# Three of four chunk outputs and their group norms moved into the state recurrence of a hybrid RWKV-7 and MLA decoder

## The chip, the core and the metric

One core of a Trainium2 chip. The metric is the device time of one execution in microseconds (us); the kernel before has a median of 1591.6 us over 3 runs (1591.0 to 1593.85). Engines are called as in the profile: PE is TensorE (PEld its weight loads), DVE is VectorE, ACT is ScalarE, POOL is GpSimd, SP is SyncE, which issues the transfers.

## The reference

Two decoder layers on 512 tokens of width 1024, then a norm. Each layer has a mixer of two branches, RWKV-7 and MLA attention, and a gated MLP. What the change touches is the RWKV branch: a state of 64x64 for each of 8 heads runs over all tokens, each token's output is read from the state, and the output is normed within its head.

```
def step(state, inp):
    r_t, w_t, k_t, v_t, a_t, b_t = inp
    sa = jnp.einsum('bhij,bhj->bhi', state, a_t)
    state = (state * w_t[:, :, None, :] + sa[..., None] * b_t[:, :, None, :]
             + v_t[..., None] * k_t[:, :, None, :])
    y_t = jnp.einsum('bhij,bhj->bhi', state, r_t)
    return state, y_t
...
mu = jnp.mean(y, axis=-1, keepdims=True)
var = jnp.mean(jnp.square(y - mu), axis=-1, keepdims=True)
y = ((y - mu) * lax.rsqrt(var + LNX_EPS)).reshape(B, S, RWKV_DIM).astype(dt) * lnx_w + lnx_b
...
return (y + bonus) * gate
```

The MLA branch is plain causal attention of 8 heads over the 512 tokens (scores, softmax, values). It doesn't depend on the recurrence; both branches meet behind their output projections.

## The kernel before

Activations lie transposed, 128 channels by 512 tokens. Every large projection is a chain of matmuls of 128x512 in three terms, high part by high part, high by low, low by high (`mm3`, L246 to L248), on weights that SP streams in and that ACT and DVE split into two parts (L201, L202). These matmuls are most of PE's work.

In each layer's mixer the 512 tokens are 8 chunks of 64. What couples tokens inside a chunk is prepared ahead (AR, AM, BT, Z). Then comes the recurrence, a loop over the chunks, c = 0 to 7, and each step is a chain between PE and DVE: PE reads the state (L785), DVE adds to `xs` (L789), PE multiplies with the chunk's inverse (L795), DVE writes the result to Z (L798), PE multiplies with BT (L804), DVE adds the decayed state from POOL (L811) to the new state `St` (L812). Between these three groups of small matmuls `filler()` puts matmuls of two projections that don't depend on the recurrence, two `mm3` at a time; it has six such pieces, which last until step 2.

Behind the loop `outputs()` forms the RWKV outputs of four chunk pairs: `chunk_out(i)` multiplies the states by AR (L833) and Z by AM (L841) into one pair of banks `xy`, and ACT copies the sum to Z (L844). `norms()` runs the group norm of each pair: DVE sum, mean and subtraction (L852 to L854), square on ACT (L855), sum and mean on DVE (L856, L857), power -0.5 on POOL (L858) and a product on POOL (L863). `transposed()` turns the four normed pairs with PE (`yop`, L869), and DVE scales and gates them (L874, L875) for the output projection. `heads(p)`, p = 0 to 3, is the attention of two heads each: scores into one of the two banks of the tag `sc` (L929), minimum on DVE (L932), exponential on ACT (L935), reciprocal on DVE (L936), scaling on ACT (L937), transposes on PE (L940) into one bank `pt`, a copy on DVE or ACT (L942), product with the values on PE (L947).

What sets the order: the recurrence is written in a block in which PE's instructions keep the order of the program among themselves. All else is ordered ahead of time by a scheduler that goes by the order of the program, by buffers and by its own costs, one fixed list for each engine; instructions of other parts of the program may be put between those of the block. So in the kernel before a good part of `heads(0)` and of the projections for it lies between the recurrence's steps 2 to 7.

```
for f in (outputs, norms, lambda: heads(0), lambda: heads(1), transposed, lambda: heads(2), lambda: heads(3)):
    f()
```

Of the kernel before, what the change touches and what calls it, by code (L numbers as in the profile page):

```python
# [9 lines left out]
F32 = mybir.dt.float32  # L10
F32R = mybir.dt.float32r
I32 = mybir.dt.int32
AF = mybir.ActivationFunctionType
# [12 lines left out]
LNX_EPS = 64e-5  # L26
# [132 lines left out]
def build(ctx, tc, x, pos, wst, vecd, constd, out):  # L159
# [265 lines left out]
    def mixer(l, ops, nrm, wks):  # L425
        with ExitStack() as mx:
# [220 lines left out]
            with pool(name=f"ti{l}", bufs=2) as ti, tc.manual_schedule(engines={PE.engine}):  # L647
# [120 lines left out]

                St = [None]
# [7 lines left out]
                for c in range(8):  # L777
# [3 lines left out]
                    if c:  # L781
# [5 lines left out]
                        filler()  # L787
# [29 lines left out]
            with pool(name=f"tb{l}", bufs=2) as tb:  # L817
# [6 lines left out]

                def chunk_out(i):
                    xy = xyt()
                    for p in range(4):
                        for e, hh in ((0, 0), (1, 1), (0, 1), (1, 0)):
                            c = 2 * i + e
                            ur, vr = rows(e)  # L830
                            k0 = 64 * hh
                            if c:
                                PE.matmul(xy[vr:vr + 64, hh, 64 * p:64 * p + 64], AR[p][k0:k0 + 64, c, vr:vr + 64],  # L833
                                          St[c][k0:k0 + 64, p, :], start=p == 0, stop=False, tile_position=(k0, vr))
                    for hh in range(2):
                        for p in range(4):
                            for e in range(2):
                                c = 2 * i + e
                                ur, vr = rows(e)
                                hd = 2 * p + hh  # L840
                                PE.matmul(xy[vr:vr + 64, hh, 64 * p:64 * p + 64], AM[:, hd, c, vr:vr + 64],  # L841
                                          Z[:, i, e, 64 * hd:64 * hd + 64], start=c == 0 and p == 0, stop=p == 3,
                                          tile_position=(0, vr))
                    A.copy(Z[:, i, 0, :].rearrange("p (q h i) -> p q h i", h=2, i=64),  # L844
                           xy[:, :, 0:256].rearrange("p h (q i) -> p q h i", i=64))


                def group_norm(i):
                    Y = Z[:, i, 0, :].rearrange("p (h i) -> p h i", i=64)
                    s2 = Z[:, i, 1, :].rearrange("p (h i) -> p h i", i=64)  # L850
                    mu = tb.tile([128, 24], F32, name="mu", bufs=4)
# [26 lines left out]
                def outputs():  # L878
                    for i in range(4):
                        chunk_out(i)  # L880
# [226 lines left out]
```

## Time and profile before

| what | value |
|---|---|
| median of 3 runs | 1591.6 us |
| profiled execution, its own time | 1593.16 us |
| its span, first to last instruction | 1591.4 us |
| PE busy | 1562.6 us, 98% |
| DVE, ACT, POOL busy | 915.4, 661.5, 184.7 us |
| recurrence, outputs and attention, layer 0 | from 236 to 354 us of the span |
| the same, layer 1 | from 1022 to 1139 us |

A row of the timeline gives the start and the length of an instruction or of a run of like ones (xN; a matmul in float32 counts as two), and in brackets how long its engine had been idle before it and what ended that. Lengths of matmuls overlap, since PE is pipelined: what a matmul costs PE is the distance from its start to the next one's.

### The profile page before, as it was taken

The page shows a single profiled execution, that of the slowest core. Times are in us where ns is not written, and L with a number is a line of the kernel's source. Part 1 is how long each engine was busy: PE and PEld are TensorE (multiplying, and loading weights), DVE is VectorE, ACT ScalarE, POOL GpSimd, SP SyncE. Part 2 cuts the span into 40 slices and gives each one's busy share as a digit, 9 for nine tenths or more (in the row PEclk, how much of TensorE's full clock was granted, in tenths as well). Part 3 has the DMA queues.
Part 4 walks back from the last instruction along what each step waited for, and adds up shares of the span by engine and source line. Part 5 has one row for each costly group of instructions (what it writes and reads, how often), then busy time and mean ns, then how long its engine had stood idle before and what let it go on. Part 6 is the DMA issues. An engine that isn't in the chain of part 4 may idle for free.

```text
span 1591.4 us, 22441 instructions
## 1 busy us (share of the span) xinstructions
PE 1562.6 (98%) x9052; PEld 1254.2 (79%) x9052; DVE 915.4 (58%) x1468; ACT 661.5 (42%) x996; POOL 184.7 (12%) x156
## 2 busy tenths in 40 slices
PE   8999999899999999999999999998999999999998
PEld 6878886668888888888878888775788888888887
DVE  6579786666555555533346668757564655554332
ACT  6445444563443333422244443446533434333222
POOL 1011102300311101100001111013002111010000
PEclk9999999999999999999999999999999999999999
DMA  5323322224423233233343233213253332332232
GB/s 192 125 100 132 121 81 67 88 74 147 123 96 99 93 97 102 93 108 120 110 146 106 94 106 120 74 48 101 86 162 103 97 102 93 95 104 93 93 104 82
DMA packets 57272, 166.08 MB, mean 104 GB/s; under 512 B 6352, under 2 KB 8528, under 8 KB 57168
## 3 DMA queue, kind: packets, MB, share of 16 engines
q1 hardware_dynamic: 57024, 164.48, 31.9%
q8 instruction: 71, 1.16, 0.3%
q14 instruction: 33, 0.27, 0.1%
q10 hardware_dynamic: 144, 0.16, 0.0%
HBM read 147.32 MB, written 17.30 MB: 103 GB/s over the span
## 4 chain that ended last, share of the span: by engine, by line
PE 91%; DVE 4%; issue 2%; ACT 1%; POOL 1%; DMA 0%; SPq 0%; POOLq 0%; DVEq 0%; ACTq 0%
PE acc L246 26%; PE acc L247 26%; PE acc L248 26%; PE sc L929 2%; PE po L947 2%; PE pt L940 1%; PE m L599 1%; PE xy L795 1%; DVE wlo L202 1%; PE m L607 1%; PE m L583 0%; PE xy L804 0%; PE m L524 0%; DVE X L661 0%; POOL mu L858 0%
## 5 line engine op out<-in xcount | busy, mean ns | idle before, releaser
L246 PE MATMUL acc<-hi,whi 128*128 128x512 f32 (+1 forms) x1910 | 752.4, 394 | 7.2 <-ACT hi L282 5.2
L248 PE MATMUL acc<-hi,wlo 128*128 128x512 f32 (+1 forms) x1910 | 742.6, 389 | 1.2 <-DVE wlo L202 1.2
L247 PE MATMUL acc<-lo,whi 128*128 128x512 f32 (+1 forms) x1910 | 742.8, 389 | 0.0
L201 ACT CAST whi<-raw 128x1024 fp32r<-128x1024 f32 (+2 forms) x249 | 253.5, 1019 | 547.2 <-PE acc L247 466.9
L246 PEld LDWEIGHTS acc<-hi,whi 128*128 128x128 f32 x1910 | 359.6, 188 | 82.5 <-ACT hi L282 5.2
L248 PEld LDWEIGHTS acc<-hi,wlo 128*128 128x128 f32 x1910 | 359.6, 188 | 76.1 <-DVE wlo L202 1.6
L247 PEld LDWEIGHTS acc<-lo,whi 128*128 128x128 f32 x1910 | 359.9, 188 | 72.4 <-issue 1.2
L202 DVE TENSOR_TENSOR wlo<-raw,whi 128x1024 fp32r<-128x1024 f32 (+2 forms) x249 | 309.5, 1244 | 175.9 <-ACT whi L201 175.5
L1027 POOL TENSOR_TENSOR c<-c,rstd 128x512 f32<-128x512 f32 x44 | 58.0, 1318 | 403.5 <-ACT c L1026 403.5
L1020 DVE TENSOR_TENSOR u<-acc,rstd 128x512 f32<-128x512 f32 x44 | 30.4, 692 | 104.7 <-PE acc L248 104.6
L1029 DVE TENSOR_TENSOR c<-c,acc 128x512 f32<-128x512 f32 x44 | 30.3, 688 | 86.4 <-POOL c L1027 86.4
L1026 ACT ACTIVATE c<-c 128x512 f32<-128x512 f32 x44 | 27.8, 632 | 81.6 <-DVE c L1025 81.6
L305 POOL TENSOR_TENSOR nv<-nv,cst 128x4 f32<-128x4 f32 (+1 forms) x10 | 10.0, 997 | 352.6 <-DVE nv L304 352.6
L341 POOL TENSOR_TENSOR nacc<-nacc,nsq 128x512 f32<-128x512 f32 x14 | 25.0, 1787 | 200.3 <-ACT nsq L340 200.3
L450 DVE TENSOR_TENSOR cur<-acc,rstd 128x512 f32<-128x512 f32 x28 | 19.1, 690 | 48.4 <-PE acc L248 39.3
L929 PE MATMUL sc<-K,q 128*128 128x128 f32 (+3 forms) x128 | 44.6, 446 | 1.1 <-DVE q L921 1.1
L935 ACT ACTIVATE P<-P,mn 128x128 f32<-128x128 f32 (+3 forms) x64 | 35.6, 556 | 17.2 <-issue 9.3
L932 DVE CUSTOM_DVE_ANT_0 P<-sc,cst 128x128 f32<-128x128 f32 (+3 forms) x64 | 30.7, 483 | 12.9 <-PE pt L940 10.4
L947 PE MATMUL po<-PT,Vt 128*64 128x128 f32 x320 | 37.5, 286 | 0.6 <-DVE PT L942 0.6
L937 ACT ACTIVATE P<-P,mn 128x128 f32<-128x128 f32 (+3 forms) x64 | 34.2, 557 | 6.6 <-DVE mn L936 6.6
L1023 ACT ACTIVATE c<-u,vec 128x512 f32<-128x512 f32 x44 | 35.7, 812 | 2.8 <-DVE u L1019 2.8
L947 PEld LDWEIGHTS po<-PT,Vt 128*64 128x64 f32 x320 | 22.3, 136 | 18.2 <-issue 7.3
(242 smaller groups left out, 1370.8 us busy)
## 6 DMA issues: line engine op xcount, KB each, us to landing
raw<-in_w SPq DMA_DIRECT2D x238, 512.0 KB, 3.4
gate_d<-gg SPq DMA_DIRECT2D x32, 256.0 KB, 2.1
AM<-gate_d SPq DMA_DIRECT2D x16, 256.0 KB, 5.9
gb<-gate_d SPq DMA_DIRECT2D x16, 256.0 KB, 3.6
h<-in_x SPq DMA_DIRECT2D x8, 256.0 KB, 4.6
rgate_d<-gt SPq DMA_DIRECT2D x8, 256.0 KB, 2.5
bl_d<-rk SPq DMA_DIRECT2D x8, 256.0 KB, 2.0
bl<-bl_d SPq DMA_DIRECT2D x8, 256.0 KB, 2.6
```

The lines of the kernel that those rows point to most:

```text
L201: A.copy(hi, r)
L202: V.tensor_tensor(lo, r, hi.bitcast(F32), ALU.subtract)
L246: PE.matmul(ps, w[0], xx[0], start=first, stop=False)
L247: PE.matmul(ps, w[0], xx[1], start=False, stop=False)
L248: PE.matmul(ps, w[1], xx[0], start=False, stop=last)
L929: PE.matmul(sp[:, 0:n], qs[hh][:, 128 * b:128 * b + 128], ks[hh][:, 0:n], start=True, stop=True)
L932: V.tensor_tensor_reduce(out=P[:, 0:n], in0=sp[:, 0:n], in1=cst[:, C_CAUS + 512 - n:C_CAUS + 512], scale=-ATT_SCALE, scalar=1e30, op0=ALU. ...
L935: A.activation(P[:, 0:n], P[:, 0:n], AF.Exp, bias=mn[:, 0:1], scale=-1.0, accum_out=mn[:, 1:2])
L937: A.activation(P[:, 0:n], P[:, 0:n], AF.Copy, scale=mn[:, 2:3])
L947: PE.matmul(po[64 * hh:64 * hh + 64, 128 * b:128 * b + 128], Vt[:, kb, 64 * hd:64 * hd + 64], PTs[hh][:, 128 * kb:128 * kb + 128], start=k ...
L1023: A.activation(cc, u[:, 2:514], AF.Identity, bias=vc(l, "conv_b", i), scale=vc(l, "conv_w", 2 * FT + i))
L1027: G.tensor_tensor(cc, cc, rstd, ALU.mult)
```

## The change

`chunk_out`, `group_norm` and `group_scale` are defined ahead of the loop. In steps 2, 4 and 6 the first of the three places for filler now takes `chunk_out(c // 2 - 1)` with its norm and scale; filler pieces that stood there move on by one place. The outputs go into two tiles of the tag `sc`, the banks that the scores of the attention use, no longer into `xy`, so ACT copies them in two halves. The tile `mu` of the norm lies in the pool `tl`. Only the last pair, 3, is left behind the loop.

```
@@ ahead of the loop, moved from behind it @@
+                def chunk_out(i):
+                    ps = [sc("co"), sc("co")]
+                    begun = set()
+
+                    def put(e, hh, p, w, x, pos, last):
+                        ur, vr = rows(e)
+                        PE.matmul(ps[hh][vr:vr + 64, 64 * p:64 * p + 64], w, x, start=(e, hh) not in begun, stop=last,
+                                  tile_position=(pos, vr))
+                        begun.add((e, hh))
+
+                    for p in range(4):
+                        for e, hh in ((0, 0), (1, 1), (0, 1), (1, 0)):
+                            c, k0 = 2 * i + e, 64 * hh
+                            vr = rows(e)[1]
+                            if c:
+                                put(e, hh, p, AR[p][k0:k0 + 64, c, vr:vr + 64], St[c][k0:k0 + 64, p, :], k0, False)
+                    for hh in range(2):
+                        for p in range(4):
+                            for e in range(2):
+                                vr = rows(e)[1]
+                                hd = 2 * p + hh
+                                put(e, hh, p, AM[:, hd, 2 * i + e, vr:vr + 64], Z[:, i, e, 64 * hd:64 * hd + 64], 0, p == 3)
+                    for hh in range(2):
+                        A.copy(Z[:, i, 0, :].rearrange("p (q h i) -> p q h i", h=2, i=64)[:, :, hh, :],
+                               ps[hh][:, 0:256].rearrange("p (q i) -> p q i", i=64))
...
+                    mu = tl.tile([128, 24], F32, name="mu", bufs=4)
...
@@ in the loop, behind L785 @@
-                        filler()
+                        if c in (2, 4, 6):
+                            chunk_out(c // 2 - 1)
+                            group_scale(c // 2 - 1, group_norm(c // 2 - 1))
+                        else:
+                            filler()
@@ behind the loop @@
                 def outputs():
-                    for i in range(4):
-                        chunk_out(i)
+                    chunk_out(3)
 
                 def norms():
-                    for i, gr in enumerate([group_norm(i) for i in range(4)]):
-                        group_scale(i, gr)
+                    group_scale(3, group_norm(3))
```

In the changed kernel the lines are: recurrence L830, L838, L844, L847, L853, L861 (before: L785, L789, L795, L798, L804, L812), chunk outputs L775 and their copies L792, norm L800 to L806 and scale L811, transposes of the outputs L877, attention L935 to L953. Three places show how the fixed orders move.

PE, from the read of the state in step 2 to the product with the inverse (`xy` is the recurrence's bank, `co` the chunk outputs, `acc` a projection). Before:

```order
L785 MATMUL xy<-St,AR_204 64x64 x2
L246 MATMUL acc<-hi,whi 128x512
L247 MATMUL acc<-lo,whi 128x512
L248 MATMUL acc<-hi,wlo 128x512
L246 MATMUL acc<-hi,whi 128x512
L247 MATMUL acc<-lo,whi 128x512
L248 MATMUL acc<-hi,wlo 128x512
L795 MATMUL xy<-xs,AM 64x64 x8
```

These two `mm3` moved on to the next place, behind the product. The same place of PE now:

```order
L830 MATMUL xy<-St,AR_204 64x64 x2
L775 MATMUL co<-St,AR_201 64x64 x2
L775 MATMUL co<-St,AR_202 64x64 x2
L775 MATMUL co<-St,AR_203 64x64 x2
L775 MATMUL co<-St,AR_204 64x64 x2
L775 MATMUL co<-Z,AM 64x64 x16
L844 MATMUL xy<-xs,AM 64x64 x8
```

The first chunk output has taken their place, so that only small matmuls stand between L830 and L844. DVE in the same steps, from the sum `xs` of step 2 to that of step 3, before:

```order
L789 TENSOR_TENSOR xs<-xy,Z 64x512
L710 TENSOR_TENSOR gg<-acc,rstd 128x512
L798 COPY Z<-xy 64x512
L202 TENSOR_TENSOR wlo<-raw,whi 128x1024
L812 TENSOR_TENSOR St<-xy,tmp 128x256
L789 TENSOR_TENSOR xs<-xy,Z 64x512
```

The next `xs` follows the state at once; the weight split stands in front of the state. DVE now:

```order
L838 TENSOR_TENSOR xs<-xy,Z 64x512
L847 COPY Z<-xy 64x512
L800 TENSOR_REDUCE mu<-Z 128x8
L710 TENSOR_TENSOR gg<-acc,rstd 128x512
L801 TENSOR_SCALAR mu<-mu 128x8
L861 TENSOR_TENSOR St<-xy,tmp 128x256
L802 TENSOR_TENSOR Z<-Z,mu 128x512
L202 TENSOR_TENSOR wlo<-raw,whi 128x1024
L804 TENSOR_REDUCE mu<-Z 128x8
L838 TENSOR_TENSOR xs<-xy,Z 64x512
```

Three operations now stand between the state and the next `xs`, where none stood.

PE, from the product with BT in step 6 to the end of the recurrence. Before:

```order
L804 MATMUL xy<-Z,BT_208 64x64 x2
L940 MATMUL pt<-cst,P 128x128 x3
L947 MATMUL po<-PT,Vt 64x128
L246 MATMUL acc<-hi,whi 128x512
L247 MATMUL acc<-lo,whi 128x512
L785 MATMUL xy<-St,AR_201 64x64 x2
```

Three pieces of other work lay between the two; they have moved. PE now:

```order
L853 MATMUL xy<-Z,BT_208 64x64 x2
L830 MATMUL xy<-St,AR_201 64x64 x2
L830 MATMUL xy<-St,AR_202 64x64 x2
L830 MATMUL xy<-St,AR_203 64x64 x2
L830 MATMUL xy<-St,AR_204 64x64 x2
L775 MATMUL co<-St,AR_201 64x64 x3
L775 MATMUL co<-St,AR_202 64x64 x4
L775 MATMUL co<-St,AR_203 64x64 x4
L775 MATMUL co<-St,AR_204 64x64 x3
L844 MATMUL xy<-xs,AM 64x64 x8
L775 MATMUL co<-St,AR_204 64x64
L775 MATMUL co<-Z,AM 64x64 x16
```

Nothing stands any more between the product with BT and the next read of the state, nor, but for the last chunk output, in step 7. DVE at the same place now:

```order
L847 COPY Z<-xy 64x512
L800 TENSOR_REDUCE mu<-Z 128x8
L801 TENSOR_SCALAR mu<-mu 128x8
L802 TENSOR_TENSOR Z<-Z,mu 128x512
L861 TENSOR_TENSOR St<-xy,tmp 128x256
L804 TENSOR_REDUCE mu<-Z 128x8
L805 TENSOR_SCALAR mu<-mu 128x8
L838 TENSOR_TENSOR xs<-xy,Z 64x512
```

The norm of pair 2 stands in front of the state and of the last `xs`.

PE, behind the recurrence, at the transpose of the last output pair (L869, now L877; `pt` are transposes of the softmax, `po` values), before:

```order
L947 MATMUL po<-PT,Vt 64x128
L940 MATMUL pt<-cst,P 128x128 x2
L869 MATMUL xy<-cst,Z 128x128
L929 MATMUL sc<-K,q 128x512 x2
L940 MATMUL pt<-cst,P 128x128 x2
```

This is the attention of `heads(1)`; that of `heads(0)` was nearly through when the recurrence ended. PE now, in the attention of `heads(0)`:

```order
L946 MATMUL pt<-cst,P 128x128 x2
L877 MATMUL xy<-cst,Z 128x128
L935 MATMUL sc<-K,q 128x512
L946 MATMUL pt<-cst,P 128x128 x2
L953 MATMUL po<-PT,Vt 64x128
L935 MATMUL sc<-K,q 128x512
```

The scores of the last block of `heads(0)` stand behind the transpose that needs the last pair's norm, and all four attention groups now lie behind the recurrence.

## Rows read from the trace of the kernel before

**Rows 1.** The page, part 1: busy time, share of the span and instructions of each engine.

```profile
PE 1562.6 (98%) x9052; PEld 1254.2 (79%) x9052; DVE 915.4 (58%) x1468; ACT 661.5 (42%) x996; POOL 184.7 (12%) x156
```

**Rows 2.** Busy time by stretch: from and to in us, length, then busy us (and instructions) of PE, PEld, DVE, ACT and POOL, the granted clock, DMA share and GB/s. The stretches are the recurrence from step 2's end, the outputs, heads(1), the rest of the attention; then the whole of it in layer 0 and in layer 1.

```profile
252.00:284.40 32.40, 31.52 (x332) 21.89 (x330) 19.19 (x48) 15.63 (x37) 6.81 (x10) 1.00 0.17 58
284.40:296.00 11.60, 10.94 (x270) 9.01 (x269) 7.36 (x15) 4.27 (x8) 5.04 (x4) 1.00 0.56 181
296.00:317.00 21.00, 17.55 (x103) 10.90 (x103) 15.27 (x44) 14.34 (x36) 7.94 (x8) 1.00 0.18 57
317.00:354.00 37.00, 37.00 (x211) 24.21 (x211) 22.70 (x72) 26.54 (x66) 0.76 (x1) 1.00 0.24 72
236.00:354.00 118.00, 112.31 (x1058) 77.51 (x1057) 72.94 (x191) 65.85 (x151) 21.78 (x24) 1.00 0.24 76
1022.00:1139.00 117.00, 111.32 (x1045) 76.70 (x1044) 73.05 (x191) 65.81 (x150) 21.79 (x24) 1.00 0.23 74
```

**Rows 3.** Timeline of PE, steps 2 and 3 of the recurrence, layer 0: start, length, line, tiles, idle time before.

```profile
248.31 0.68 PE L785 MATMUL xy<-St,AR 64*64 64x64 f32 x16
...
250.18 0.40 PE L248 MATMUL acc<-hi,wlo 128*128 128x512 f32 x1
250.51 1.14 PE L795 MATMUL xy<-xs,AM 64*64 64x64 f32 x16
251.58 0.50 PE L903 MATMUL acc<-whi,hi 128*128 128x512 f32 x1
251.92 0.39 PE L903 MATMUL acc<-whi,lo 128*128 128x512 f32 x1
252.15 0.40 PE L903 MATMUL acc<-wlo,hi 128*128 128x512 f32 x1
...
253.17 0.69 PE L804 MATMUL xy<-Z,BT 128*64 128x64 f32 x16
254.45 0.68 PE L785 MATMUL xy<-St,AR 64*64 64x64 f32 x16 [0.60 <-DVE St L812]
...
255.92 1.14 PE L795 MATMUL xy<-xs,AM 64*64 64x64 f32 x16
```

**Rows 4.** Timeline of PE, the first chunk outputs behind the recurrence, layer 0.

```profile
284.45 0.68 PE L833 MATMUL xy<-St,AR 64*64 64x64 f32 x16
285.06 1.15 PE L841 MATMUL xy<-Z,AM 128*64 128x64 f32 x32
286.14 0.66 PE L940 MATMUL pt<-cst,P 128*128 128x128 f32 x4
...
287.09 0.69 PE L833 MATMUL xy<-St,AR 64*64 64x64 f32 x32
```

**Rows 5.** Timeline of DVE in step 2, layer 0.

```profile
249.04 0.69 DVE L789 TENSOR_TENSOR xs<-xy,Z 64x512 f32<-64x512 f32 x1 [1.71 <-PE xy L785]
...
251.69 0.69 DVE L798 COPY Z<-xy 64x512 f32<-64x512 f32 x1 [0.38 <-PE xy L795]
252.41 1.23 DVE L202 TENSOR_TENSOR wlo<-raw,whi 128x1024 fp32r<-128x1024 f32 x1
253.97 0.43 DVE L812 TENSOR_TENSOR St<-xy,tmp 128x256 f32<-128x256 f32 x1 [0.33 <-PE xy L804]
```

**Rows 6.** Timeline, the group norm of pair 0 on DVE, ACT and POOL, layer 0.

```profile
286.90 0.69 DVE L852 TENSOR_REDUCE mu<-Z 128x8 f32<-128x512 f32 x1 [1.66 <-ACT Z L844]
...
287.90 0.69 DVE L854 TENSOR_TENSOR Z<-Z,mu 128x512 f32<-128x512 f32 x1
289.35 0.69 DVE L856 TENSOR_REDUCE mu<-Z 128x8 f32<-128x512 f32 x1 [0.76 <-ACT Z L855]
...
288.68 0.63 ACT L855 ACTIVATE Z<-Z 128x512 f32<-128x512 f32 x1 [1.26 <-DVE Z L854]
...
290.38 1.64 POOL L858 TENSOR_TENSOR mu<-mu,cst 128x8 f32<-128x8 f32 x1 [16.35 <-DVE mu L857]
292.10 1.04 POOL L863 TENSOR_TENSOR Z<-Z,mu 128x512 f32<-128x512 f32 x1
```

**Rows 7.** Timeline of PE, steps 6 and 7, layer 0: the recurrence's own groups, between which other matmuls run without a gap.

```profile
278.19 0.69 PE L804 MATMUL xy<-Z,BT 128*64 128x64 f32 x16
...
280.31 0.68 PE L785 MATMUL xy<-St,AR 64*64 64x64 f32 x16
...
282.20 1.14 PE L795 MATMUL xy<-xs,AM 64*64 64x64 f32 x16
```

**Rows 8.** Timeline of PE, the transposes of the outputs that waited, layer 0.

```profile
296.82 0.41 PE L869 MATMUL xy<-cst,Z 128*128 128x128 f32 x2 [0.61 <-ACT Z L844]
...
300.55 0.33 PE L869 MATMUL xy<-cst,Z 128*128 128x128 f32 x1 [1.16 <-POOL Z L863]
```

**Rows 9.** Groups of instructions, whole span, of the softmax: busy us, mean ns of one, idle time before.

```profile
L935 ACT ACTIVATE P<-P,mn 128x128 f32<-128x128 f32 (+3 forms) x64 | 35.6, 556 | 17.2 <-issue 9.3
L932 DVE CUSTOM_DVE_ANT_0 P<-sc,cst 128x128 f32<-128x128 f32 (+3 forms) x64 | 30.7, 483 | 12.9 <-PE pt L940 10.4
L937 ACT ACTIVATE P<-P,mn 128x128 f32<-128x128 f32 (+3 forms) x64 | 34.2, 557 | 6.6 <-DVE mn L936 6.6
```

**Rows 10.** Timeline of POOL and of DVE, a product on POOL and a weight split on DVE at the same time, layer 0.

```profile
299.45 1.04 POOL L863 TENSOR_TENSOR Z<-Z,mu 128x512 f32<-128x512 f32 x1
...
299.78 1.79 DVE L202 TENSOR_TENSOR wlo<-raw,whi 128x1024 fp32r<-128x1024 f32 x1
```

More of the change, by code (lines that the diff above doesn't have):

```diff
@@ new lines, in group_norm @@
+                def group_norm(i):
+                    Y = Z[:, i, 0, :].rearrange("p (h i) -> p h i", i=64)
+                    s2 = Z[:, i, 1, :].rearrange("p (h i) -> p h i", i=64)
+                    mu = tl.tile([128, 24], F32, name="mu", bufs=4)
+                    V.tensor_reduce(mu[:, 0:8], Y, mybir.AxisListType.X, ALU.add)
+                    V.tensor_scalar(mu[:, 0:8], mu[:, 0:8], 1.0 / 64, None, ALU.mult)
+                    V.tensor_tensor(Y, Y, mu[:, 0:8, None].to_broadcast([128, 8, 64]), ALU.subtract)
+                    A.activation(s2, Y, AF.Square)
+                    V.tensor_reduce(mu[:, 8:16], s2, mybir.AxisListType.X, ALU.add)
+                    V.tensor_scalar(mu[:, 8:16], mu[:, 8:16], 1.0 / 64, LNX_EPS, ALU.mult, ALU.add)
+                    G.tensor_tensor(mu[:, 16:24], mu[:, 8:16], mhalf[:, 0:8], ALU.pow)
+                    return mu[:, 16:24]
@@ L769, in mixer, with group_scale @@
+                def group_scale(i, gr):
+                    Y = Z[:, i, 0, :].rearrange("p (h i) -> p h i", i=64)
+                    G.tensor_tensor(Y, Y, gr[:, :, None].to_broadcast([128, 8, 64]), ALU.mult)
                 St = [None]
@@ L822, in mixer @@
                 kvop = split(xp, lat[2], None, "xa", 8)
[L825 to L845, printed above, removed]
@@ L848, in group_norm @@
[L848 to L851, printed above, removed]
-                    V.tensor_reduce(mu[:, 0:8], Y, mybir.AxisListType.X, ALU.add)
-                    V.tensor_scalar(mu[:, 0:8], mu[:, 0:8], 1.0 / 64, None, ALU.mult)
-                    V.tensor_tensor(Y, Y, mu[:, 0:8, None].to_broadcast([128, 8, 64]), ALU.subtract)
-                    A.activation(s2, Y, AF.Square)
-                    V.tensor_reduce(mu[:, 8:16], s2, mybir.AxisListType.X, ALU.add)
-                    V.tensor_scalar(mu[:, 8:16], mu[:, 8:16], 1.0 / 64, LNX_EPS, ALU.mult, ALU.add)
-                    G.tensor_tensor(mu[:, 16:24], mu[:, 8:16], mhalf[:, 0:8], ALU.pow)
-                    return mu[:, 16:24]
@@ L861, in group_scale @@
-                def group_scale(i, gr):
-                    Y = Z[:, i, 0, :].rearrange("p (h i) -> p h i", i=64)
-                    G.tensor_tensor(Y, Y, gr[:, :, None].to_broadcast([128, 8, 64]), ALU.mult)
                 yops = []
```

## The prediction, made before the changed kernel ran

> **What bounds the kernel now.** I read the busy times first: PE works 98% of the span [rows 1], so a change that moves work without adding any can win only what PE idles, or what it loses in passing from one kind of matmul to another. Next the stretches that the change touches [rows 2]: the reader takes PE's busy time from the length of each. In layer 0 PE idles 32.40 - 31.52 = 0.88 us in the recurrence from step 2 on, 11.60 - 10.94 = 0.66 us in the outputs, 21.00 - 17.55 = 3.45 us in heads(1) and nothing in the rest: 4.99 us. Over the whole stage it is 118.00 - 112.31 = 5.69 us, in layer 1 117.00 - 111.32 = 5.68 us, so what holds for one layer holds for both. Everything the change could win by filling waits is therefore some 10 us of 1591.6. The timelines [rows 3 to 10] then price the steps.
>
> **What moves.** By the two orders, PE has the same matmuls in this stage. Pairs 0 to 2 of the outputs go into steps 2, 4 and 6, and for want of score banks heads(0) goes from the recurrence to behind it. So the sum consists of waits gained and lost and of changes of kind.
>
> **Waits that go.** In the recurrence from step 2 the 0.88 us go, of which 0.60 us is the wait for the state of step 3 [rows 3]: four of the value matmuls now stand there.
>
> **Chunk output in its place.** It costs PE 0.61 us for the states (16 or 32 rows take the same, 284.45 to 285.06) and 1.08 us for Z (285.06 to 286.14) [rows 4], together 1.69 us. The xs that it covers is ready 0.73 + 0.69 + 0.06, about 1.5 us after L830's start (248.31 to 249.04, then its length) [rows 3, 5]. So steps 2, 4 and 6 are covered there, and PE is the later one by 0.8 us (0.61 + 1.69 - 1.5).
>
> **A new wait in step 3.** I walk DVE's new row from L830 of step 2 as zero. L844 starts at 2.30, Z at 3.48 (1.18 behind, as 250.51 to 251.69 [rows 3, 5]), the six matmuls end and L853 starts at 4.96, the state starts 0.80 later (253.17 to 253.97 [rows 3, 5]), at about 5.9 behind the gate product, and ends at 6.3. PE, with four value matmuls (1.13), begins L830 of step 3 at 6.71 and has two more matmuls until 7.99. DVE in the meantime has the subtraction (0.60 start to start), the weight split of 1.23 us [rows 5], of which 1.14 count, and the second sum (0.69 [rows 6]) before xs: xs starts at about 8.65 and ends at 9.35. PE waits 9.40 - 7.99, less what the ends overlap: **1.35 us**. Before, L785 to L795 of this step were 254.45 to 255.92 with hardly a gap [rows 3].
>
> **New waits in steps 6 and 7.** Here DVE has the sum, the mean and the subtraction before the state. By rows 6 the subtraction starts 1.00 us after the sum (286.90 to 287.90) and gives DVE free some 0.60 later; the sum starts 0.60 after Z. The state so starts 2.2 us after Z's start instead of when PE delivers, and PE, with nothing between L853 and L830, waits 0.9 us. The square on ACT ends 2.4 us after the sum's start (286.90, 288.68 + 0.63), the second sum and mean follow, xs is late: PE waits 0.6 us more before L844. Then it waits for Z of step 7 with only three small matmuls left: 1.18 + 0.69 - 1.14 - 0.05 is 0.7 us. Together **2.2 us**; before, these places ran without a gap (278.19, 280.31 and 282.20 are bridged by other matmuls [rows 7]).
>
> **Behind the recurrence.** The 0.66 and 3.45 us of before go as far as they were waits for the outputs (0.61 for the copy, 1.16 for the product on POOL [rows 8], the rest mostly for softmax steps). New is that heads(0) starts with an empty pipeline: one softmax is at the mean 0.48 on DVE and 0.56 and 0.56 on ACT [rows 9] besides two passes of PE, in single file, with two score banks. The norm of pair 3 takes 6.24 us from the sum's start to the product's end (286.90 to 292.10 + 1.04 [rows 6]) and cannot start until 2.0 us after Z of step 7 (chunk output 1.0, copies 0.7, a score in DVE's row before it); three softmax pieces that stand between its parts add about 0.9 us. So the transpose L877 of pair 3 can run at about 9.1 us, and all behind it waits. PE has until then 0.95 us of the chunk output, 0.4 of transposes, six scores of about 3.1, and 1.4 of transposes and values: 5.9 us. It idles **3.2 us**, 2 of them in front of L877. I add 0.5 us for the rest of heads(0) and 1.0 for heads(1) to heads(3), nearest to the 1.1 us that remain in heads(1) of before once both transposes have run (3.45 less the gaps up to 302 us). That is 4.7 against 4.1 us: **+0.6**. Bounds: nothing if fillers cover as in the last 37 us of rows 2, and 4.1 more if each of heads(0)'s softmax steps stands bare.
>
> **Changes of kind.** Matmuls of 128x512 follow each other by 0.23 us (251.92 to 252.15); before a small group it is 0.33 (250.18 to 250.51) and the first one behind is 0.34 (251.58 to 251.92) [rows 3]. So each visit of big matmuls between small ones costs 0.21 us. From step 2 to the last output I count 19 such visits before and 11 now: **-1.7 us**. From the state part to the Z part of a chunk output, another tile shape, no such cost shows: 0.61 us [rows 4]. [...]
>
> **What costs nothing.** The norm's other operations are the same number on the same engines. ACT copies halves, some 0.15 us more each, under PE's work. Transfers: the gate loads into AM need only pairs 0 and 1 and so start earlier; one weight load stands behind the first of them on SP's queue, and its weights are split only near the end of heads(0): covered. Product and power on POOL stand before two of the state's decays, which are ready 4 us early. POOL and DVE do hinder each other: the weight split took 1.79 instead of 1.23 us beside a product on POOL [rows 5, 10]. Here the products fall beside xs and Z, so I take 0, at most 0.56 per layer.
>
> **Sum.** Per layer -0.88 + 1.35 + 2.2 + 0.6 - 1.7 = +1.57 us, twice +3.1 us. The profiled execution took 1593.16 us (span 1591.4), so 1596.3; that execution lies 1.6 us above the median, so I forecast **1594.7** for the median. About 0.2%, 3.2 us, is what can be told from no change, so the forecast is at the edge: its own range is 1590.5 to 1598.5 and lies half on either side.
>
> **Rivals.**
> 1. *Faster: the outputs' waits vanish.* If heads(0) flows as well as the 37 us without a gap in rows 2, and the norm of pair 3 is ready before PE comes to its transpose, only 1.0 us of idle remains behind the recurrence in place of 4.7. Per layer 1.57 - 3.7 = -2.1, in all 4.3 below the median: 1587.3. It decides if pair 3 is normed by 7 us behind Z of step 7. For it: three of four norms are out of the way and the copies no longer chain. Against: the norm is one row of dependent operations, 6.24 us, with softmax steps between. Chance 0.12.
> 2. *Clearly slower: heads(0) bare.* In heads(1) of before PE idled 3.45 of 21 us with projections beside it; heads(0) now has six big matmuls. If it idles as much again on top, per layer +3.3, in all 3.1 + 6.6: 1601.3. For it: ACT was 14.34 us busy in those 21. Against: no q work and only one norm are left there. Chance 0.18.
> 3. *Nothing to see.* The waits of steps 3, 6 and 7 come out as large as what the visits and the old waits give back; PE's 98% leaves no more. 1591.6. Chance 0.10.
>
> **Chances.** The forecast has 0.60, half of it over the bound. Faster by over 0.2%: 0.10, from rival 1 (its rest, 0.02, is no change). Within: 0.30 + 0.02 + 0.10 + 0.01 = 0.43. Slower: 0.30 + 0.17 = 0.47. The range reaches to the middle of rival 1 and of rival 2: 1587.5 to 1601.0, some 0.15 left out.
>
> **What would show it.** Right: in each layer PE waits for xs about 1.3 us in step 3, for the state 0.9 us in step 7's read, for xs and Z 0.6 and 0.7 us, and about 2 us for the product on POOL in front of L877; the recurrence ends about 1 us earlier than now and the attention about 1.5 us later; the idle of the stage grows by about 3.3 us per layer while PE's busy time falls. Wrong: no wait in front of L877 or a step-3 wait under 0.5 us (then rival 1), or an idle share behind the recurrence above 8 us (rival 2).

## The result, and the profile after

| | before | after |
|---|---|---|
| median | 1592.55 us (1591.0 to 1593.85, 6 runs) | 1599.74 us (1598.18 to 1602.77, 6 runs) |
| ratio after / before | | 1.0047, 95% interval 1.0037 to 1.0058 |
| profiled execution, its span | 1593.16, 1591.4 us | 1599.89, 1598.1 us |
| mean granted clock of TensorE | 0.997 | 0.993 |

Slower by 7.2 us (by the interval 5.9 to 9.2), where 3.1 us were forecast. The waits that I had walked by hand are there, each within 0.3 us; most of the loss is a thing that my sum did not contain: TensorE's clock. Busy times of after, page part 1 (compare [rows 1]):

```profile
PE 1567.4 (98%) x9052; PEld 1258.5 (79%) x9052; DVE 914.2 (57%) x1468; ACT 662.9 (41%) x1004; POOL 185.2 (12%) x156
```

PE has the same number of matmuls and is busy 4.8 us longer. The timeline of PE shows the new waits, layer 0: steps 2 and 3, then steps 6 and 7, then the transpose of pair 3 (compare [rows 3, 4, 7, 8]).

```profile
248.36 0.68 PE L830 MATMUL xy<-St,AR 64*64 64x64 f32 x16
248.88 0.63 PE L775 MATMUL co<-St,AR 64*64 64x64 f32 x16
249.44 1.15 PE L775 MATMUL co<-Z,AM 128*64 128x64 f32 x32
250.52 1.14 PE L844 MATMUL xy<-xs,AM 64*64 64x64 f32 x16
...
254.93 0.68 PE L830 MATMUL xy<-St,AR 64*64 64x64 f32 x16
257.81 1.83 PE L844 MATMUL xy<-xs,AM 64*64 64x64 f32 x16 [1.53 <-DVE xs L838]
261.57 1.12 PE L853 MATMUL xy<-Z,BT 128*64 128x64 f32 x16
264.20 0.77 PE L830 MATMUL xy<-St,AR 64*64 64x64 f32 x10
...
282.23 0.51 PE L830 MATMUL xy<-St,AR 64*64 64x64 f32 x10 [1.15 <-DVE St L861]
284.00 0.97 PE L844 MATMUL xy<-xs,AM 64*64 64x64 f32 x13 [0.63 <-DVE xs L838]
285.92 1.15 PE L775 MATMUL co<-Z,AM 128*64 128x64 f32 x28 [0.40 <-DVE Z L847]
294.43 0.33 PE L877 MATMUL xy<-cst,Z 128*128 128x128 f32 x1 [1.49 <-POOL Z L811]
```

Look at the lengths in step 3: L844 takes 1.83 us at 257.81 and 1.14 at 250.52, L853 1.12 where it took 0.69 [rows 3]. The same step in layer 1, with the same wait in front:

```profile
1046.83 1.14 PE L844 MATMUL xy<-xs,AM 64*64 64x64 f32 x16 [1.54 <-DVE xs L838]
1049.04 0.69 PE L853 MATMUL xy<-Z,BT 128*64 128x64 f32 x16
1050.55 0.51 PE L830 MATMUL xy<-St,AR 64*64 64x64 f32 x10
```

Here L844 to the next L830 takes 3.72 us, in layer 0 it took 6.39. DVE's row ahead of that wait (compare [rows 5]):

```profile
253.99 0.42 DVE L861 TENSOR_TENSOR St<-xy,tmp 128x256 f32<-128x256 f32 x1
254.33 0.68 DVE L802 TENSOR_TENSOR Z<-Z,mu 128x512 f32<-128x512 f32 x1
254.93 1.64 DVE L202 TENSOR_TENSOR wlo<-raw,whi 128x1024 fp32r<-128x1024 f32 x1
256.49 0.67 DVE L804 TENSOR_REDUCE mu<-Z 128x8 f32<-128x512 f32 x1
257.08 0.67 DVE L838 TENSOR_TENSOR xs<-xy,Z 64x512 f32<-64x512 f32 x1
```

Busy time by stretch of after (columns as in [rows 2], the granted clock is the third number from the end). First step 3 in the two layers just compared (the window of layer 0 ends 0.5 us after the next read has begun); then step 0 to the read of step 7 and from there to the last value product of heads(3), in layer 0 and in layer 1.

```profile
257.80:264.70 6.90, 6.89 (x50) 5.07 (x52) 1.14 (x3) 1.79 (x3) 5.04 (x6) 0.51 0.41 146
1046.83:1050.55 3.72, 3.72 (x40) 2.71 (x40) 1.14 (x3) 0.91 (x2) 3.55 (x4) 1.00 0.74 268
...
235.70:282.23 46.53, 43.16 (x572) 32.96 (x571) 26.05 (x43) 13.94 (x24) 13.63 (x15) 0.93 0.34 112
282.23:356.92 74.69, 71.14 (x487) 46.34 (x487) 46.21 (x148) 52.52 (x131) 8.43 (x9) 1.00 0.17 50
1024.72:1068.42 43.70, 40.26 (x571) 30.83 (x570) 26.10 (x43) 13.92 (x24) 13.64 (x15) 1.00 0.34 111
1068.42:1145.36 76.94, 73.83 (x487) 48.78 (x487) 46.36 (x148) 52.63 (x131) 8.43 (x9) 0.96 0.16 48
```

And the same two parts of before, layer 0, then what follows to step 0 of layer 1, before and after:

```profile
235.64:280.31 44.67, 43.10 (x432) 30.52 (x431) 26.15 (x58) 18.99 (x41) 8.04 (x12) 1.00 0.21 70
280.31:353.91 73.60, 69.48 (x631) 47.26 (x630) 46.79 (x134) 46.81 (x110) 13.74 (x12) 1.00 0.26 80
353.91:1021.02 667.11, 664.74 (x3417) 544.64 (x3417) 375.61 (x513) 256.35 (x331) 69.61 (x51) 1.00 0.34 109
```
```profile
356.92:1024.72 667.80, 665.42 (x3421) 545.14 (x3421) 375.65 (x513) 256.45 (x331) 69.61 (x51) 1.00 0.34 109
```

Each part of after occurs once at full clock (1.00) and once with a stretch at a granted clock of 0.50 in it, at different places in the two layers: behind step 3's wait in layer 0 (258 to 264 us), behind the waits of step 7 in layer 1 (1072 to 1076 us). So the low clock can be priced within one profile: 46.53 - 43.70 = 2.83 us in layer 0 and 76.94 - 74.69 = 2.25 us in layer 1, **5.1 us** in all. Without it the stage takes 43.70 + 74.69 = 118.39 us against 44.67 + 73.60 = 118.27, and 0.69 us (one `mm3`) has slipped behind heads(3): **+0.81 us per layer**. 5.1 + 2 x 0.81 is 6.7 us, the difference of the two spans. This is read from one execution of each kernel; that it is no accident of this one is seen from the mean clocks of all six, 0.991 to 0.994, against 0.997 to 0.999 in the executions of the kernel before that were timed beside the experiments.

### The profile page after: what moved, and what is told of

Read it like the earlier page. It is cut to its first block, busy times and chain, and to the rows that moved or that the text cites. A ratio compares the mean times of both kernels' runs of the same rounds, so it can differ in the third digit from the quotient of the medians.

```text
span 1598.1 us, 22446 instructions
## 1 busy us (share of the span) xinstructions
PE 1567.4 (98%) x9052; PEld 1258.5 (79%) x9052; DVE 914.2 (57%) x1468; ACT 662.9 (41%) x1004; POOL 185.2 (12%) x156
## 4 chain that ended last, share of the span: by engine, by line
PE 91%; DVE 4%; issue 2%; ACT 1%; POOL 1%; DMA 0%; SPq 0%; POOLq 0%; DVEq 0%; ACTq 0%
PE acc L246 26%; PE acc L248 26%; PE acc L247 26%; PE sc L935 2%; PE po L953 2%; PE pt L946 1%; PE m L599 1%; DVE wlo L202 1%; PE xy L844 1%; PE co L775 1%; PE m L607 1%; PE m L583 0%; PE m L524 0%; DVE X L661 0%; POOL mu L806 0%
## 5 line engine op out<-in xcount | busy, mean ns | idle before, releaser
L935 PE MATMUL sc<-K,q 128*128 128x128 f32 (+3 forms) x128 | 45.5, 457 | 0.4 <-DVE mn L938 0.3
L953 PEld LDWEIGHTS po<-PT,Vt 128*64 128x64 f32 x320 | 22.2, 136 | 23.9 <-issue 6.4
L953 PE MATMUL po<-PT,Vt 128*64 128x128 f32 x320 | 36.7, 286 | 0.8 <-DVE PT L948 0.8
```

Source lines behind the costliest of these rows:

```text
L935: PE.matmul(sp[:, 0:n], qs[hh][:, 128 * b:128 * b + 128], ks[hh][:, 0:n], start=True, stop=True)
L953: PE.matmul(po[64 * hh:64 * hh + 64, 128 * b:128 * b + 128], Vt[:, kb, 64 * hd:64 * hd + 64], PTs[hh][:, 128 * kb:128 * kb + 128], start=k ...
```

## The experiments

Theory A: DVE's new row makes the waits, and the waits let TensorE's clock fall; the low clock is most of the loss. B: waits cost what they last, the low clock only accompanies them. C: the attention pushed behind the recurrence is what costs. Ratios are against the kernel before, with their 95% interval.

### The waits filled: e1_warm

```
@@ in the loop, ahead of the read of step 7 (4), and behind the read in steps 3 (5) and 7 (2)
+    dm = sc("dm")
+    for _ in range(n):
+        PE.matmul(dm, ops[0][0][:, 0:128], ops[0][0], start=True, stop=True)
```

> The changed kernel with matmuls added whose results nothing reads: five of 128x512 between the state's read and the product with the inverse in step 3, four between the product with BT of step 6 and the read of step 7, two behind that read, in a bank of their own. They take 11 x 0.23 = 2.5 us per layer and stand where PE waited 1.53, 1.15 and 0.63 us. Theory A (the new waits let TensorE's clock fall once per layer, and the low clock costs 2.95 us in layer 0 and 2.27 us in layer 1): the clock stays at 1.00 in both layers, and the time is 1599.7 - 5.2 = 1594.5 us, up to 1 us more if the added matmuls do not quite fit. Theory B (the waits and the displaced attention alone cost the 7 us, the low clock only slows work that would have waited anyway): the time stays at 1599.7 us or rises by up to 1 us.

1595.74 us (1.0021, 1.0012 to 1.0029): 4.0 us less than the changed kernel, of 5.2 expected, with eleven more matmuls per layer. Step 3, read to read, takes 6.59 us at clock 1.00 in layer 0 and 6.58 in layer 1; in the changed kernel it was 264.20 - 254.93 = 9.27 us in layer 0 and 6.60 in layer 1. The timeline of PE in step 3, layer 0, then busy time by stretch: step 3, behind the recurrence in layer 0, ahead of that of layer 1:

```profile
253.95 1.45 PE L818 MATMUL dm<-hi 128*128 128x512 f32 x5
256.22 1.14 PE L852 MATMUL xy<-xs,AM 64*64 64x64 f32 x16 [0.37 <-DVE xs L846]
```
```profile
253.34:259.93 6.59, 6.22 (x64) 4.49 (x63) 4.01 (x7) 2.60 (x5) 5.65 (x6) 1.00 0.58 199
288.00:294.00 6.00, 4.51 (x13) 1.95 (x13) 2.92 (x10) 3.19 (x9) 2.64 (x3) 0.72 0.00 1
1020.00:1024.00 4.00, 3.92 (x23) 2.84 (x24) 1.37 (x2) 0.66 (x1) 0.00 (x0) 0.57 0.41 135
```

Where matmuls filled the waits the clock held at 1.00 (in step 3 of both layers, and in layer 1 from the read of step 7 to the wait for pair 3, 1067.01 to 1079.61 us). It fell elsewhere instead: behind the unfilled wait of 1.49 us for pair 3 in layer 0 (not behind the same wait in layer 1, where the clock is 1.00 from 1067.01 to 1142.08 us), and ahead of the recurrence of layer 1, a place that the change does not touch. From 0.72 over 6 us and 0.57 over 4 us I estimate at most 1.7 us for each of these two. That is more than the missing 1.2 us; the rest was not separated.

### The norms left out: e2_no_norm and e3_before_no_norm

```
@@ e2: changed kernel, in the loop      @@ e3: kernel before, norms()
-    group_scale(..., group_norm(...))  -    for i, gr in enumerate(...): group_scale(i, gr)
                                        +    group_scale(3, group_norm(3))
```

> The changed kernel without the group norms of pairs 0 to 2, which are left out of the computation; the chunk outputs stay in steps 2, 4 and 6 and the attention of the first two heads behind the recurrence. Theory A with the norm's operations on DVE as the cause of the waits: the waits of steps 3 and 6/7 (1.53, 1.15, 0.63 us) go but for about 0.3 us each, the clock stays at 1.00, and the time falls by 5.2 + 2 x 2.4 = 10 us to 1589.7 us. If the clock falls without these waits too (for want of large matmuls in steps 2, 6 and 7): 1599.7 - 4.8 = 1594.9 us. Theory C (the cost is the attention that was pushed behind the recurrence): the time stays above 1597 us.

> The kernel before without the group norms of pairs 0 to 2, as a control for the run without them of the changed kernel. The norms stand behind the recurrence beside other work there; what they can cost is the wait of the transposes for the product on POOL, 1.16 us in layer 0. Theory A and C alike: 1592.5 us less 0 to 2.5 us. The difference of the two kernels without norms is then what moving the chunk outputs is worth by itself: A expects the changed one to be level with or below this one, C some 5 us above it.

e2: 1591.37 us (0.9995, 0.9986 to 1.0004); e3: 1587.89 us (0.9971, 0.9960 to 0.9982), some 4 us below the kernel before, where at most 2.5 were expected; why was not looked into. Without the norms step 3 has no wait (254.44 to 255.90, as before the change) and no low clock (1.00 from 248.40 to 255.90 us, and behind it the product with BT takes 0.69 us, as in [rows 3]): the norm was the cause. C as it was put falls, since e2 has the whole displaced attention and is level with the kernel before. But the control for e2 is e3, and e2 is still 3.5 us above it, where A had expected it level. From step 0 of layer 0 to step 0 of layer 1 it takes 784.91 us, e3 782.76. Both layers of e2 have the low clock behind the wait of 1.48 us for pair 3, and e3 has none in the stage. Busy time by stretch of e2, from the transpose of pair 3 on:

```profile
288.51:294.00 5.49, 5.49 (x20) 2.76 (x21) 2.19 (x6) 2.84 (x8) 1.22 (x2) 0.69 0.03 9
...
1073.41:1079.00 5.59, 5.58 (x21) 2.81 (x22) 2.25 (x7) 2.83 (x8) 1.22 (x2) 0.69 0.11 20
```

From 0.69 instead of 1.00 I estimate at most 0.31 x 5.5 = 1.7 us for each of these two, about the 3.5 us. The wait for pair 3 stands behind the recurrence, among the displaced attention, so a part of C remains: it has a price here, but was not tested by itself.

### Two pairs only: e4_two_pairs

```
-    if c in (2, 4, 6):
+    if c in (2, 4):          # and pairs 2 and 3 behind the loop
```

> The changed kernel with only pairs 0 and 1 in the recurrence (steps 2 and 4); pair 2 goes behind the loop beside pair 3, still in the score banks, and by the fixed order its matmuls then stand in steps 6 and 7, between the product with BT and the read of the state. DVE's row of step 3 is unchanged, that of step 6 has no mean and subtraction in front of the last state. Theory A: the wait of 1.53 us in step 3 stays, and in layer 0 the fall of the clock behind it; the waits of steps 6 and 7 (1.15, 0.63) go, and in layer 1 the clock does not fall there: 1599.7 - 2 x 1.8 - 2.3 = 1593.8 us, or 1596 us if the clock falls behind step 3 in layer 1 instead. Theory C (displaced attention): the attention stays behind the recurrence, so no change beyond 1 us, 1599 us.

1600.12 us (1.0050, 1.0037 to 1.0063): a miss for A's number, and near C's 1599, but with five falls of the clock in its trace, which C has no place for (the execution traced is the slowest of the five). Step 3's wait of 1.53 us stayed, and this time the clock fell behind it in both layers (0.67 over 5.2 us), again behind the recurrence in both (0.72 over 6 us) and once ahead of the recurrence of layer 1 (0.66 from 1020 to 1030 us). I had assumed that a fall sits at one place per layer; it does not.

### The norm placed by hand: e5_norm_by_hand, e6_hand_warm_late

```
+    pieces = {(3, 0): (0,), (3, 1): (0,), (4, 0): (0,), (5, 0): (1,), ...}   # (step, gap): pair
+    with tc.manual_schedule(engines={PE.engine, V.engine}):                  # DVE held in this order too
...
@@ e6 besides: six dm products in step 7, and in transposed(), all of i < 3 ahead of i == 3
+    for i, q in [(i, q) for i in range(3) for q in range(2)] + [(3, 0), (3, 1)]:
```

> The changed kernel with DVE's order in the recurrence written by hand, so that at most one large operation of a norm stands in each gap between the recurrence's own: sum of pair 0 behind xs of step 3, subtraction behind Z of step 3, second sum behind xs of step 4, and so on; pair 2 in step 7. Chunk outputs and the displaced attention stay as in the changed kernel. Theory A (the row of the norm's operations ahead of the state and of xs makes the waits, and the waits let the clock fall): the wait of 1.53 us in step 3 shrinks to 0.3 us or less, 1.15 us before the read of step 7 to about 0.6; layer 0 shows no low clock behind step 3. That is 2 x (1.2 + 0.5) = 3.4 us of waits and the low clock of 2 to 5 us: 1591 to 1594.5 us, and the low clock may come back behind the recurrence, at the wait of 1.49 us for pair 3. Theory C (the displaced attention costs it): within 1 us of 1599.7 us.

> The kernel with the norm's operations placed by hand, and two additions: six matmuls of 128x512 that nothing reads in step 7 (four ahead of the read of the state, two behind it), and the transposes of pair 3 of the first two blocks put behind those of pairs 0 to 2. Theory A: the waits of step 3 and of step 7 go, the wait for pair 3 (1.49 us) falls to 0.5 us or less, the clock stays at 1.00 in both layers. Without low clock the changed kernel's stage was 0.13 us longer than that of before (117.30 against 117.17); less 1.3 + 0.9 + 0.8 us of waits it is 2.9 us shorter per layer: 1592.0 - 5.8 = 1586.2 us, under 1589 us in any case, so faster than before. Theory C: not below the kernel before, 1592 us or more.

e5: 1597.74 us (1.0035, 1.0023 to 1.0047), e6: 1600.6 us (1.0049, 1.0037 to 1.0062), both well above what A gave. In e5 the wait for xs in step 3 is gone and layer 0 has no low clock, as expected (the product with BT of step 3 takes 0.69 us, as in [rows 3]). But holding all of DVE put the gate product (L710), which itself waits for PE, ahead of the state of step 1 and, with a weight split behind it, ahead of that of step 3: PE waits 1.21 and 0.86 us for them, in the kernel before nothing and 0.60. And the wait in front of the transposes moved from pair 3 to pair 2, whose norm now ends behind the recurrence: POOL's product of pair 2 runs from 286.01 us for 1.04 us, and the transpose that needs it at 287.10 us, after a wait of 1.65 us; pair 3 waits no more. The clock fell ahead of layer 1's recurrence (0.57 from 1018 to 1026 us). In e6 it is pair 2 again that waits, 1.50 us, and pair 3 another 0.53, with waits of 0.48 and 0.74 us for the softmax behind them; in layer 1 the clock fell there (0.57 from 1076 to 1084 us), and once some 33 us ahead of the recurrence (0.72 from 990 to 996 us). What part of the 14 us by which e6 missed is which was not separated.

### One wait added to the kernel before: e8_before_wait, e9_before_wait_warm, e10_before_short_wait

```
@@ kernel before, in the loop, behind L789
+    for _ in range(2 if c == 1 else 0):        # e10: 1
+        V.tensor_tensor(xs[ur:ur + 64], xs[ur:ur + 64], xs[ur:ur + 64], ALU.max)
@@ e9 besides: behind the filler of step 1, twelve products that nothing reads
+    PE.matmul(dm, ops[0][0][:, 0:128], ops[0][0], start=True, stop=True)
```

> The kernel before with two more DVE operations in place on xs in step 1 (the maximum of xs with itself, 64x512 each), nothing else; PE's order is the same. PE's wait of 0.69 us in front of the product with the inverse grows by about 1.2 us to 1.9 us in each layer; on both sides of it PE has its full row of large matmuls. Theory A in its strict form (a wait of 1.5 us or more lets the clock fall by itself): the low clock shows behind step 1 and the time is 1592.0 + 2 x (1.2 + 2.5) = 1599.4 us. Theory A in its weaker form (it takes the wait and a stretch of small matmuls around it): the clock stays at 1.00 and the time is 1592.0 + 2.4 = 1594.4 us. Theory B: 1594.4 us as well.

> As the run of the kernel before with two added DVE operations in step 1, and now twelve matmuls of 128x512 that nothing reads on PE in the same place, behind its large matmuls and ahead of the product with the inverse. DVE's chain is unchanged, so the product starts no earlier; PE is only kept working for 12 x 0.23 = 2.8 us of the 3.22 us that it waited there. Theory A (the wait lets the clock fall, and the low clock has a price of its own): no low clock behind step 1 in either layer, and the time falls from 1601.2 us by the low clock's 1.5 us in layer 0 and 2.5 us in layer 1 (the excess of steps 1 and 2 over the longer wait), to 1597.2 us; the wait's 2 x 2.5 us stay. Theory B (waiting alone costs the time): 1601 us or more.

> The kernel before with one added DVE operation on xs in step 1 in place of two: half the dose. With two the wait grew from 0.69 to 3.22 us; with one I expect about 1.9 us (0.69 + 1.25), near the 1.53 us of the changed kernel's step 3. Theory A: if 1.9 us is enough the low clock shows behind step 1 in at least one layer and the time is 1592 + 2.5 + 2 to 4 = 1597 to 1599 us; if it is not, 1594.5 us. Theory B: 1594.5 us.

e8: 1601.17 us (1.0059, 1.0046 to 1.0072); e9: 1597.17 us (1.0031, 1.0020 to 1.0043); e10: 1598.49 us (1.0034, 1.0021 to 1.0046). First e8, the product of step 1 in both layers and the window from the read of step 1 to that of step 2, which takes 7.80 us in the kernel before:

```profile
244.32 1.42 PE L797 MATMUL xy<-xs,AM 64*64 64x64 f32 x16 [3.22 <-DVE xs L792]
...
1034.68 1.94 PE L797 MATMUL xy<-xs,AM 64*64 64x64 f32 x16 [3.21 <-DVE xs L792]
```
```profile
238.84:250.68 11.84, 8.62 (x67) 6.26 (x66) 6.83 (x10) 3.42 (x5) 0.61 (x1) 0.86 0.19 66
1029.20:1041.98 12.78, 9.57 (x67) 7.16 (x66) 6.83 (x10) 3.42 (x5) 0.61 (x1) 0.73 0.18 62
```

The wait grew by 2.53 us, twice what I had expected, since two splits of latents came to stand between the added operations. The steps grew by 4.04 and 4.98: 1.5 and 2.5 us are the low clock's. Then e9, the timeline of layer 0 and the same two windows, with PE kept at work:

```profile
241.08 2.88 PE L791 MATMUL dm<-hi 128*128 128x512 f32 x12
243.92 1.11 PE L801 MATMUL xy<-xs,AM 64*64 64x64 f32 x16
```
```profile
238.97:248.76 9.79, 9.79 (x80) 7.49 (x79) 7.00 (x10) 3.47 (x5) 0.61 (x1) 1.00 0.23 80
1026.69:1036.48 9.79, 9.79 (x80) 7.49 (x79) 7.00 (x10) 3.48 (x5) 0.61 (x1) 1.00 0.23 82
```

No low clock in them, and 4.0 us less in all, at the forecast value: B falls. The two windows are 2.05 and 2.99 us shorter than in e8. Some 1.1 us of that are not the clock's, because one of those splits now stands behind the two added operations and xs came 0.53 us sooner per layer; so the clock accounts for about 4 us in the windows and about 3 of the 4.0 in the median. Last e10, the same two views, where the same wait stands in both layers:

```profile
243.22 1.79 PE L797 MATMUL xy<-xs,AM 64*64 64x64 f32 x16 [1.96 <-DVE xs L792]
...
1032.77 1.11 PE L797 MATMUL xy<-xs,AM 64*64 64x64 f32 x16 [1.95 <-DVE xs L792]
```
```profile
239.00:251.06 12.06, 10.10 (x67) 7.52 (x66) 6.23 (x9) 3.41 (x5) 0.61 (x1) 0.72 0.18 65
1028.55:1037.61 9.06, 7.11 (x67) 5.24 (x66) 6.23 (x9) 3.42 (x5) 0.61 (x1) 1.00 0.24 87
```

In layer 0 the clock fell behind it, in layer 1 it did not: 3.00 us between two runs of the same instructions. So behind one and the same wait it fell once, at 1.96 us, and once not, at 1.95 us.

### Other orders of the transposes and of DVE: e7_before_late, e11_hand_from_3, e12_hand_transposes_late

```
@@ e7: kernel before with the order of transposes of e6
@@ e11: e5 with DVE held from step 3 on only
+    with tc.manual_schedule(engines={PE.engine, V.engine} if c >= 3 else {PE.engine}):
@@ e12: e11, and in heads(1) behind its second q: the bank of the transposes is held until then
+    PE.matmul(xyt()[:, 0, 0:128], ks[0][:, 0:128], qs[1][:, 0:128], start=True, stop=True)
```

> The kernel before with only the transposes of pair 3 put behind those of pairs 0 to 2, a control for the same step in the run beside it. Both theories: the waits of 0.61 us for the copy and 1.16 us for the product on POOL in front of the transposes shrink or move; between no change and 2 x 1.7 us less: 1588.6 to 1592.0 us. If this one is as fast as the run beside it, the gain there owes nothing to the outputs inside the recurrence.

> The changed kernel with the norm's operations placed by hand, as in the earlier run, but with DVE's order held by hand only from step 3 on, so that the weight splits of steps 0 to 2 stand where they stood in the changed kernel. The earlier run's stage in layer 0 was 116.56 us from the first product of step 0 to the last value matmul of heads(3), 118.27 us in the kernel before; 1.28 us of it was a new wait for the state of step 1, and step 2 to 3 took 8.11 us where the changed kernel takes 6.57. Theory A: stage about 114.5 us where no low clock falls into it, so 2 x 3.8 = 7.6 us less than before plus whatever low clock there is: 1584.5 to 1590 us, faster than both kernels. Theory C (the attention pushed behind the recurrence costs the time): not below the kernel before, 1592 us.

> The run with the norm placed by hand from step 3 on, and in addition the transposes of the outputs held back until the second query block of heads(1) is there (one added product of 128x128 on the transposes' bank that nothing reads, behind which they stand). In the run before it PE waited 0.28, 0.72 and 1.65 us between the recurrence and the transpose of pair 3, and in layer 1 the clock fell there. Theory A: the wait of 1.65 us goes, some of it comes back as waits for the softmax of heads(0), since the transposes of pairs 0 to 2 no longer stand between its steps; the stage takes 113.5 us, up to 114.7 if all of it comes back (114.65 before), and no low clock shows between 1065 and 1085 us. Time: 1593.7 - 2 x 1.1 - 1.5 = 1590 us, 1587 to 1593; faster than both kernels if under 1589.5. Rival: the softmax of heads(0) stands bare, waits of over 2 us per layer take the place of the one removed, and the low clock stays: 1593.5 us or more.

e7: 1588.97 us (0.9986, 0.9977 to 0.9995). Its two waits in front of the transposes are still there (0.60 and 1.15 us), so my reason for it was wrong; PE idles 3.10 instead of 4.12 us between the read of step 7 and the end of heads(3), since the fixed order of heads(1) came out different. From step 0 of layer 0 to step 0 of layer 1 it takes 785.24 us, with one low stretch outside of the stage (0.76 from 985 to 992 us), against 785.38 us without one in the kernel before. Which part of that order pays was not looked into.

e11: 1593.71 us (1.0007, 0.9998 to 1.0016), level with before, not faster, where 1584.5 to 1590 were expected. Step 0 to step 7's read takes 41.60 us against 44.67 and 43.70, and steps 2 to 6 have no wait any more; but PE waits 0.28, 0.72 and 1.65 us behind the recurrence, the last again for pair 2, and in layer 1 the clock falls there (0.72 from 1072 to 1078 us), and once some 33 us ahead of the recurrence (0.50 from 988 to 990 us).

e12: 1589.66 us (0.9983, 0.9974 to 0.9992). PE's longest waits from step 7 on, layer 0, and the time from step 0 of layer 0 to step 0 of layer 1:

```profile
277.97 0.51 PE L837 MATMUL xy<-St,AR 64*64 64x64 f32 x10 [0.60 <-DVE St L869]
...
281.36 1.15 PE L775 MATMUL co<-Z,AM 128*64 128x64 f32 x28 [0.40 <-DVE Z L854]
283.53 0.89 PE L950 MATMUL sc<-K,q 128*128 128x128 f32 x4 [0.48 <-DVE mn L953]
285.08 0.70 PE L950 MATMUL sc<-K,q 128*128 128x256 f32 x2 [0.66 <-DVE mn L953]
```
```profile
236.38:1020.13 783.75, 776.89 (x4480) 622.91 (x4479) 447.31 (x704) 322.87 (x485) 90.87 (x75) 1.00 0.31 104
```

No wait over 0.7 us, and no low clock behind the recurrence in either layer (1.00 from 277.97 to 292 and from 1061.88 to 1076 us). The time from layer to layer is 783.75 us, 785.38 in the kernel before and 789.02 in the changed one. So the outputs inside the recurrence need not cost anything, once the norm's operations stand in DVE's gaps and nothing waits long. That they pay is not shown: e7, which leaves them behind the loop, is as fast, and the kernel before with its transposes held back as in e12 was not run.

## Why the prediction was right in sign and half in size

- **Step 3's wait:** 1.35 us forecast, 1.53 and 1.54 measured. I had taken the price of POOL beside DVE at 0, because the products fall elsewhere, and named 0.56 as the bound [rows 10]. The products did, but the weight split met two other operations of POOL, the state's decay (254.49 us, 0.99 long) and a cast (255.43 us, 1.60 long), and took 1.64 us against 1.23 [rows 5]. Most of these 0.4 us were made up, since the state started 253.99 - 248.36 = 5.63 us behind L830, in my walk at about 5.9.
- **Steps 6 and 7:** 0.9, 0.6, 0.7 forecast; 1.15, 0.63, 0.40 measured, 2.18 against 2.2. The read of step 7 comes 43.70 us behind step 0 against 44.67, 1.0 us earlier, as forecast.
- **Behind the recurrence:** the wait for pair 3 was 1.49 us, forecast about 2. But I put 1.5 us on top for what follows it, and there PE idles 0.3 us: from the read of step 7 on PE idles 74.69 - 71.14 = 3.55 us at full clock, forecast 0.6 + 0.7 + 4.7 = 6.0. Idle over the stage grew by 1.3 us per layer, not by 3.3.
- **Changes of kind:** -1.7 forecast; PE's busy time in the stage fell by 1.18 us at full clock, and 0.69 of it only moved behind heads(3): -0.49. This term was more than three times too large. I had found no cost between two small shapes, and that reading was wrong. The kernel before has the Z part in front of matmuls of its own shape too, where it costs 0.98 us:

```profile
287.72 1.15 PE L841 MATMUL xy<-Z,AM 128*64 128x64 f32 x32
288.70 0.83 PE L947 MATMUL po<-PT,Vt 128*64 128x128 f32 x12
```

  In front of another shape it costs 1.08 us, before the change (285.06 to 286.14 [rows 4]) and now in front of L844 (249.44 to 250.52), so such a change costs 0.10 us. What makes up the rest of the 1.2 us that this term missed by was not measured.
- **What failed:** the sum "-0.88 + 1.35 + 2.2 + 0.6 - 1.7 = +1.57 us" has no term for the clock. I had read 1.00 in every stretch of [rows 2] and taken it as given, though I was adding three waits of about a microsecond among small matmuls. The waits and visits came to +0.81 us per layer, half of my sum, and the clock to 2.5 us per layer, which I had at nothing. The two errors have opposite signs. Even so the median of 1599.74 us lies above the forecast's own range, 1590.5 to 1598.5; it lies inside the wider one, up to 1601.0, which had been drawn for rival 2's waits. That the wider one held is luck.
- **Rivals:** heads(0) did not stand bare (3.55 us of idle behind the read of step 7, under the 8 us that I had set as the mark), and its 1601.3 us would have looked like a good guess for the wrong cause. What the first rival supposes, a norm that is ready before PE comes to its transposes, is seen in e12, where no transpose waits, but there the norms were placed by hand and the transposes held back. The third, nothing to see, is excluded by the interval.

## What to carry to other kernels

Read the granted clock of each stretch beside its idle time, and before adding a wait to a tuned stretch ask what the next few microseconds cost at a low clock (at 0.51 step 3 took 6.39 us from L844 to the next read, at 1.00 it took 3.72): here a change that cost 1.6 us by its waits, less what it saved, brought 5.1 us of low clock with it. When operations move into a chain, count not how busy their engine is but how much fits into each gap of the chain; one large DVE operation per gap left no wait in steps 3 to 6 (e11), three in a row cost 1.5 us. And where a wait can't be removed, matmuls that nothing reads can keep the price at the wait itself, as in step 3 of e1 and in the windows of e9, where the clock stayed at 1.00.

## What the runs showed of the hardware

- The clock's fall is not a fixed consequence of a wait: it fell behind 1.96 us of waiting in layer 0 of e10 (0.72) and not behind 1.95 us in layer 1 (1.00), behind 1.49 us for pair 3 in layer 0 of e1 (0.72) and not in layer 1 (1.00), and behind 1.53 us in both layers of e4 (0.67) but only in layer 0 of the changed kernel (0.51; behind 1.54 us in layer 1 it was 1.00).
- My estimates above take a low stretch's price to be at most its length times what its clock lacks of 1.00. For 6.90 us at 0.51 in layer 0 of the changed kernel that estimate is 3.4 us; the difference of the layers is 2.83, less: nothing in that window took quite twice as long. L844 took 1.76 us to the next matmul (257.81 to 259.57) against 1.07 in layer 1, L853 1.05 against 0.61, and matmuls of 128x512 followed each other by 0.42 us against 0.23.
- The low clock also came where no kernel here changed anything. It came just ahead of layer 1's recurrence (e1: 0.57 from 1020 to 1024 us, e4: 0.66 from 1020 to 1030 us, e5: 0.57 from 1018 to 1026 us), where PE had run groups of 32x32 matmuls and waited up to 0.81 us with no releaser that the profile shows. And it came some 33 us ahead of a recurrence with no wait of PE at all, in e12 at 204 us and in layer 1 of e6, e7 and e11 (from 991, 986 and 987 us; 0.72 from 990 to 996 us, 0.76 from 985 to 992 us and 0.50 from 988 to 990 us), each time behind a run of 64x64 matmuls (x32) and one of 128x1 (x16). The timeline of PE in e12, then busy time by stretch:

```profile
201.29 1.15 PE L696 MATMUL xy<-Z,AM 64*64 64x64 f32 x32
202.36 1.95 PE L325 MATMUL sc<-cst,lsq 128*128 128x1 f32 x16
```
```profile
203.00:210.00 7.00, 7.00 (x35) 6.01 (x35) 4.72 (x12) 2.41 (x4) 1.34 (x2) 0.76 0.22 76
```

  At the same place of e12's layer 1, and of both layers of the kernel before, it did not fall (1.00 from 984 to 996 us, and from 200 to 210 and from 985 to 997 us). So a wait is not the only thing that stands ahead of a fall; what decides stays open.
- Executions of one kernel differ in their clock, and their time goes with it: e11 from 1589.39 us at a mean clock of 0.999 to 1596.80 at 0.993, e12 from 1587.53 at 0.999 to 1593.95 at 0.995. A trace is one execution, so the places of the falls in it are one case among several; kernels are compared by their medians.
